# Five places for the short convolution of a hybrid decoder layer, and one sum taken from a transfer to VectorE

## The chip, the cores and the metric

The kernel runs on one core of a Trainium2 chip. The metric is the device time of one execution in microseconds (us), the median over several runs. Five engines work side by side: TensorE (PE in the profile, its weight loads PEld), VectorE (DVE), ScalarE (ACT), GpSimd (POOL) and SyncE (SP), which issues most transfers. Each engine works through its own instructions in the order in which the program wrote them; an instruction that waits holds up all that stands behind it on that engine.

## What is computed

One decoder layer over 256 positions of 2048 channels: a norm, a mixer, a second norm and a feed-forward part, with scales and shifts from a conditioning vector. The mixer's part that is changed here is the short gated convolution:

```python
proj = h @ w_in                      # cb, cc, cx, q, k, v, r, a_lr
y_conv = cb * causal_dwconv3(cc * cx, conv_w)
o = gla_chunked(q, k, v, log_a)      # gated linear attention
o = rmsnorm(o, gla_norm_w) * silu(r)
y = concat([y_conv, o]) @ w_out
```

`causal_dwconv3` adds, per channel, three taps: position t times w2, position t-1 times w1, position t-2 times w0.

## The kernel before

Matrix products are made in split precision: each fp32 weight tile `raw` that arrives is copied by ACT to a rounded tile `wh` (line 138), DVE subtracts to get the rest `wl` (line 143), and TensorE adds the products of the high and low parts. A *unit* is one weight tile with its products. `drive` walks through all units in one fixed order that is written out by hand. For unit i it issues: the steps hung on `early`; `prep` of unit i+2 (the transfer of its weights on SP, the `wh` copy on ACT); `low` of unit i+1 (the `wl` subtraction on DVE); the steps on `pre`; the products of unit i on TensorE (`mm`); the steps on `mid`; the sums of unit i-1's banks (`fin`, function `evac`); and the steps on `late`.

The products with `w_in` are made in four chunks of input channels. This case is about the last chunk and what follows, which the code calls `tail`: t0 to t17 are the units of the last `w_in` chunk, t18 to t25 and t26 to t33 those of `w_out`. Units t12, t13, t14 and t17 have two column tiles, the other `w_in` units here three. `wh` has 3 buffers, `wl` 3, `raw` 6: the `wh` copy for unit i+3 waits for the products of unit i.

In `tail` these steps share the engines:

- `evac` of the last chunk: a finished pair of column tiles is added to what the earlier chunks left in `proj`. Most pairs are added by DVE from the bank (line 443). Pairs of cc, cx and v go another way: ACT copies the bank to a tile `hf` (line 440) and POOL issues an adding transfer to `proj` (line 441). Pairs 9 and 10 (both of cx) are summed in t11. Pair 11 is summed in t14.
- The linear attention: one level of scores per unit; `outputs` on TensorE at the start of t15; `norms` at the end of t15, eight squares with sums on ACT (line 368, bank of 256 columns) and a square root (line 738) that needs a table load; `scaled` in the `pre` of t16, a reciprocal on DVE (line 743) and eight scaled copies on ACT (line 748).
- `conv_pair(i)`, i from 0 to 3, with u = 9, 12, 13, 15. At the end of unit u, `first`: cc times cx on DVE (line 551), then the two copies scaled by tap 2 on ACT (line 553). In the `pre` of u+1, `second`: four shifted multiply-adds on DVE (line 134, 128x255 and 128x254), the product with cb (line 560) and its rounded copy on ACT (line 562). At the end of u+1 (u+2 for i = 3), `third`: the low part on DVE (line 566).
- `mod_steps`: multiply-adds of conditioning weights on DVE (line 134 with `macc`, 128x2048), one in most units.
- From t17 on, `turn`, `gate` and `gate_low`, which bring the attention's output to the form that `w_out` needs.

In the `pre` of t16, `scaled` was hung before the convolution's step, and stands ahead of it. A convolution pair i is first used by unit t18+i.

Of the kernel before, what the change touches and what calls it, by code (L numbers as in the profile page):

```python
# [24 lines left out]
CHUNKS = (2, 4, 5, 5)  # L25
# [17 lines left out]
BY_DMA = ("cc", "cx", "v")  # L43
# [58 lines left out]
def layer_kernel(ctx: ExitStack, tc, x, c, w_mod, b_mod, mix_pre_w, mix_post_w, w_in, conv_w, gate_w2, gate_b,  # L102
                 gla_norm_w, w_out, ffn_pre_w, ffn_post_w, w_up, ffn_conv_w, w_down, ident_in, masks_in, out):
    nc = tc.nc
# [12 lines left out]
    def nm(s):  # L117
        uid[0] += 1
        return f"{s}_{uid[0]}"

    def slot(shape, dt=F32):
        return big.tile(shape, dt, tag="big", name=nm("big"))
# [10 lines left out]
    def stt(o, a, s, b, op0=ALU.mult, op1=ALU.add):  # L133
        nc.vector.scalar_tensor_tensor(o, a, s, b, op0=op0, op1=op1)  # L134
# [90 lines left out]
    def conv_c(k, o):  # L225
        return sv[:, 32 + k * 8 + o:33 + k * 8 + o]
# [175 lines left out]
    def hf_tile():  # L402
        return wts.tile([P, 2, T], F32, tag="hf", name=nm("hf"), bufs=NHF)
# [15 lines left out]
    proj = {}  # L419
# [7 lines left out]
    def evac(ci, pair, ps):  # L427

        name = names[pair // 2]
        if name not in proj:  # L430
            proj[name] = slot([P, 4, T])
        dst = proj[name][:, (pair % 2) * 2:(pair % 2) * 2 + 2, :]
        if pair not in written:
            written.add(pair)
            nc.scalar.activation(dst, ps, AF.Copy, scale=QS if name == "q" else 1.0)
        elif name == "q":
            stt(dst, ps, QS, dst)
        elif ci == len(CHUNKS) - 1 and name[:-1] in BY_DMA:
            away_sum = hf_tile()
            nc.scalar.copy(away_sum, ps)  # L440
            nc.gpsimd.dma_start(dst, away_sum, accum_op=ALU.add)
        else:
            nc.vector.tensor_add(dst, dst, ps)
# [33 lines left out]
    def in_units(ci):  # L477
# [16 lines left out]
        def unit(tiles, plain):  # L494
# [37 lines left out]
            def fin():  # L532
                for p in dict.fromkeys(nt // 2 for nt in tiles):
                    done[p] = done.get(p, 0) + sum(nt // 2 == p for nt in tiles)
                    if done[p] == 2 and p not in keep:
                        evac(ci, p, banks[p])
# [6 lines left out]
    mts = {}  # L543

    def conv_pair(i):

        s = slice((i % 2) * 2, (i % 2) * 2 + 2)

        def first():
            cb, cc, cx = (proj[n + str(i // 2)][:, s, :] for n in ("cb", "cc", "cx"))  # L550
            nc.vector.tensor_mul(cc, cc, cx)
            for j in range(2):
                nc.scalar.activation(cx[:, j, :], cc[:, j, :], AF.Copy, scale=conv_c(2, 2 * i + j))

        def second():
            cb, cc, cx = (proj[n + str(i // 2)][:, s, :] for n in ("cb", "cc", "cx"))
            for tap, d in ((1, 1), (0, 2)):
                for j in range(2):
                    stt(cx[:, j, d:], cc[:, j, :T - d], conv_c(tap, 2 * i + j), cx[:, j, d:])
            nc.vector.tensor_mul(cb, cb, cx)  # L560
            mts[i] = slot([P, 2, 2, T], F32R)
            nc.scalar.copy(mts[i][:, :, 0, :], cb)

        def third():
            cb = proj["cb" + str(i // 2)][:, s, :]
            nc.vector.tensor_sub(mts[i][:, :, 1, :], cb, mts[i][:, :, 0, :].bitcast(F32))

        return first, second, third


    flat = lambda a: a.rearrange("p h t -> p (h t)")
# [503 lines left out]
    for ci in range(1, len(CHUNKS)):  # L1075
        n, us = CHUNKS[ci], chunks[ci - 1]
# [20 lines left out]
    tail = chunks[-1] + owait  # L1097
# [48 lines left out]
    for e in range(4):  # L1146
        tail[GATE[e] - 1].late.append(lambda e=e: turn(e))
    for i, u in enumerate(CONV):
        c0, c1, c2 = conv_pair(i)
        tail[u].late.append(c0)  # L1150
        tail[u + 1].pre.append(c1)
        tail[u + (1 if i < 3 else 2)].late.append(c2)
    owait[8].late.append(warm_sqrt)
    for t in range(2):
        owait[XRE + t].late.append(lambda t=t: load_x(t))
# [212 lines left out]
def build(nc, tc_args=None, arrays=None):  # L1368
    import concourse.tile as _tile

    args = []
    for name, a in arrays.items():
        args.append(nc.dram_tensor(f"in_{name}_dram", a.shape, mybir.dt.from_np(a.dtype), kind="ExternalInput").ap())
    for i, (shape, dtype) in enumerate(_OUTS):
        args.append(nc.dram_tensor(f"out_{i}_dram", shape, getattr(mybir.dt, dtype), kind="ExternalOutput").ap())
    with _tile.TileContext(nc, **(tc_args or {})) as tc:
        with tc.manual_schedule():
            layer_kernel(tc, *args)
# [13 lines left out]
```

## Time and profile before

| | |
|---|---|
| time, median of 3 runs | 1212.24 us (1211.05 to 1212.39) |
| the profiled execution's own time | 1211.78 us |
| its span, first to last instruction | 1210.0 us |
| PE busy | 1173.6 us (97%) |
| DVE busy | 937.0 us (77%) |
| ACT busy | 579.2 us (48%) |
| POOL busy | 45.6 us (4%) |
| granted TensorE clock, mean | 0.999 |

A share of busy time says little here: the `tail` lies between some 241 and 448 us of the span, and what an edit there is worth shows only in the stretches of that part, in who waits for whom.

### The profile page before, as it was taken

The numbers are of one execution on the slowest core, as the hardware profiler recorded it, in microseconds if no ns is written. First come the engines' busy times: TensorE is split into PE (matmuls) and PEld (weight loads), VectorE is DVE, ScalarE is ACT, GpSimd is POOL, SyncE is SP. The second block draws the span as 40 slices with busy tenths as digits, with TensorE's granted clock in tenths as the row PEclk, the third lists the DMA queues.
The fourth block names the chain that finished last, engine by engine and source line by source line (L and its number), as shares of the span: only waits on it lengthen the run. The fifth ranks groups of instructions, "written<-read, shape, count | busy, mean of one in ns | idle before, by whom it ended". The sixth has DMA issues, their size and how long they took to land.

```text
span 1210.0 us, 17230 instructions
## 1 busy us (share of the span) xinstructions
PE 1173.6 (97%) x7038; PEld 1038.3 (86%) x7038; DVE 937.0 (77%) x946; ACT 579.2 (48%) x675; POOL 45.6 (4%) x64
## 2 busy tenths in 40 slices
PE   2999999999999999999999999999999999999997
PEld 1999999999987888888888888888888888888885
DVE  5989899999999778884598979797976664545463
ACT  5563423454573547344554544544544543443442
POOL 2000020001101001000000000000000000000000
PEclk9999999999999999999999999999999999999999
DMA  9999899998899877996566767768664675555522
GB/s 301 387 391 390 305 384 400 399 361 266 235 336 373 330 282 284 345 375 213 174 217 238 276 220 256 254 212 296 224 230 153 226 261 180 202 191 191 198 80 70
DMA packets 128463, 323.88 MB, mean 268 GB/s; under 512 B 8502, under 2 KB 34566, under 8 KB 118657
## 3 DMA queue, kind: packets, MB, share of 16 engines
q1 hardware_dynamic: 124048, 312.63, 72.2%
q0 software_dynamic: 4048, 10.08, 3.2%
q8 instruction: 55, 0.90, 0.3%
q14 instruction: 24, 0.19, 0.0%
q10 hardware_dynamic: 288, 0.07, 0.0%
HBM read 315.42 MB, written 4.19 MB: 264 GB/s over the span
## 4 chain that ended last, share of the span: by engine, by line
PE 87%; DVE 4%; DMA 4%; issue 3%; ACT 1%; POOL 0%; SPq 0%; DVEq 0%; ACTq 0%; POOLq 0%
PE ps L936 27%; PE ps L938 14%; PE ps L793 9%; PE ps L794 9%; PE ps L792 9%; PE ps L525 5%; PE ps L527 5%; PE ps L526 5%; DMA raw<-in_w_mod_dram 2%; DVE big L134 1%; DVE wl L143 1%; PE ps L296 1%; DMA big<-hf 1%; PE ps L463 1%; DVE macc L134 1%
## 5 line engine op out<-in xcount | busy, mean ns | idle before, releaser
L138 ACT CAST wh<-raw 128x2048 fp32r<-128x2048 f32 (+3 forms) x203 | 370.1, 1826 | 502.9 <-PE ps L936 187.3
L143 DVE TENSOR_TENSOR wl<-raw,wh 128x2048 fp32r<-128x2048 f32 (+3 forms) x203 | 443.3, 2186 | 147.7 <-ACT wh L138 147.6
L936 PE MATMUL ps<-big,wh 128*128 128x512 f32 x1400 | 494.9, 399 | 0.0
L938 PE MATMUL ps<-big,wl 128*128 128x256 f32 x1400 | 393.1, 281 | 0.0
L936 PEld LDWEIGHTS ps<-big,wh 128*128 128x128 f32 x1400 | 263.0, 188 | 64.7
L938 PEld LDWEIGHTS ps<-big,wl 128*128 128x128 f32 x1400 | 264.5, 189 | 0.0
L527 PE MATMUL ps<-big,wl 128*128 128x256 f32 x768 | 218.7, 285 | 3.0 <-DVE wl L143 2.9
L525 PE MATMUL ps<-big,wh 128*128 128x256 f32 x768 | 220.4, 287 | 0.2 <-ACT wh L138 0.2
L526 PE MATMUL ps<-big,wh 128*128 128x256 f32 x768 | 218.3, 284 | 0.0
L134 DVE SCALAR_TENSOR_TENSOR macc<-raw,c_act,macc 128x2048 f32<-128x2048 f32 (+1 forms) x96 | 199.9, 2083 | 2.8 <-DMA raw<-in_w_mod_dram 2.6
L792 PE MATMUL ps<-wh,big 128*128 128x512 f32 x456 | 178.4, 391 | 0.0
L793 PE MATMUL ps<-wl,big 128*128 128x512 f32 x456 | 177.7, 390 | 0.4 <-DVE wl L143 0.3
L794 PE MATMUL ps<-wh,big 128*128 128x512 f32 x456 | 177.5, 389 | 0.0
L527 PEld LDWEIGHTS ps<-big,wl 128*128 128x128 f32 x768 | 148.3, 193 | 3.9 <-DVE wl L143 3.9
L525 PEld LDWEIGHTS ps<-big,wh 128*128 128x128 f32 x768 | 148.4, 193 | 2.7 <-ACT wh L138 1.4
L526 PEld LDWEIGHTS ps<-big,wh 128*128 128x128 f32 x768 | 148.4, 193 | 0.0
L793 PEld LDWEIGHTS ps<-wl,big 128*128 128x128 f32 x456 | 85.6, 188 | 18.8 <-DVE wl L143 1.0
L794 PEld LDWEIGHTS ps<-wh,big 128*128 128x128 f32 x456 | 85.6, 188 | 17.9
L792 PEld LDWEIGHTS ps<-wh,big 128*128 128x128 f32 x456 | 85.6, 188 | 17.7 <-issue 0.2
L134 DVE SCALAR_TENSOR_TENSOR big<-big,fcw,big 128x254 f32<-128x254 f32 (+1 forms) x176 | 72.4, 489 | 0.0
L862 DVE TENSOR_TENSOR big<-big,ps 128x256 f32<-128x256 f32 x88 | 31.1, 417 | 48.0 <-ACT big L860 48.0
L882 ACT ACTIVATE big<-big,fcw 128x256 f32<-128x256 f32 x88 | 37.9, 516 | 16.2 <-DVE big L873 16.2
(199 smaller groups left out, 649.5 us busy)
## 6 DMA issues: line engine op xcount, KB each, us to landing
raw<-in_w_up_dram SPq DMA_DIRECT2D x88, 1024.0 KB, 5.6
raw<-in_w_mod_dram SPq DMA_DIRECT2D x64, 1024.0 KB, 7.4
raw<-in_w_down_dram SPq DMA_DIRECT2D x44, 1024.0 KB, 4.8
raw<-in_w_in_dram SPq DMA_DIRECT2D x28, 960.0 KB, 9.2
raw<-in_w_mod_dram SPq DMA_DIRECT2D x32, 640.0 KB, 7.8
raw<-in_w_out_dram SPq DMA_DIRECT2D x16, 1024.0 KB, 7.7
raw<-in_w_in_dram SPq DMA_DIRECT2D x12, 1024.0 KB, 8.7
raw<-in_w_mod_dram SPq DMA_DIRECT2D x22, 512.0 KB, 8.3
```

The source lines that it names most:

```text
L134: nc.vector.scalar_tensor_tensor(o, a, s, b, op0=op0, op1=op1)
L138: nc.scalar.copy(hi, raw)
L143: nc.vector.tensor_sub(lo, raw, hi.bitcast(F32))
L525: nc.tensor.matmul(ps, w[0][:, kk, cs], ht[:, k % 2, 0, :], start=st, stop=False)
L526: nc.tensor.matmul(ps, w[0][:, kk, cs], ht[:, k % 2, 1, :], start=False, stop=False)
L527: nc.tensor.matmul(ps, w[1][:, kk, cs], ht[:, k % 2, 0, :], start=False, stop=sp)
L792: nc.tensor.matmul(ps, a[:, i, 0, ts_], w[0][:, kk, ns], start=st, stop=False)
L793: nc.tensor.matmul(ps, a[:, i, 0, ts_], w[1][:, kk, ns], start=False, stop=False)
L794: nc.tensor.matmul(ps, a[:, i, 1, ts_], w[0][:, kk, ns], start=False, stop=sp)
L882: nc.scalar.activation(st["c"][:, o, :], st["u"][o], AF.Copy, scale=fcw[:, 2, ch + o:ch + o + 1])
L936: nc.tensor.matmul(pss[o], wh[:, kk, cs], h2[k // 2][:, k % 2, :, :], start=(first and kk == 0), stop=False)
L938: nc.tensor.matmul(pss[o][:, 1, :], wl[:, kk, cs], h2[k // 2][:, k % 2, 0, :], start=False, stop=(last and kk == 3))
```

## The change

The convolution's three steps become five. `first` keeps only the product of cc and cx. The two tap copies on ACT become `tap`, in the `pre` of u+1, ahead of `second`. The rounded copy on ACT becomes `high_part`, at the end of u+1. `third`, the low part, stands at the end of u+2 for all four pairs. And in the last chunk pair 10 is added by DVE from its bank, without the copy and the transfer.

```diff
-        elif ci == len(CHUNKS) - 1 and name[:-1] in BY_DMA:
+        elif ci == len(CHUNKS) - 1 and name[:-1] in BY_DMA and pair != 10:
...
             nc.vector.tensor_mul(cc, cc, cx)
+
+        def tap():
+            cc, cx = (proj[n + str(i // 2)][:, s, :] for n in ("cc", "cx"))
             for j in range(2):
                 nc.scalar.activation(cx[:, j, :], cc[:, j, :], AF.Copy, scale=conv_c(2, 2 * i + j))
...
             nc.vector.tensor_mul(cb, cb, cx)
+
+        def high_part():
             mts[i] = slot([P, 2, 2, T], F32R)
-            nc.scalar.copy(mts[i][:, :, 0, :], cb)
+            nc.scalar.copy(mts[i][:, :, 0, :], proj["cb" + str(i // 2)][:, s, :])
...
-        return first, second, third
+        return first, tap, second, high_part, third
...
-        c0, c1, c2 = conv_pair(i)
-        tail[u].late.append(c0)
-        tail[u + 1].pre.append(c1)
-        tail[u + (1 if i < 3 else 2)].late.append(c2)
+        first, tap, second, high_part, third = conv_pair(i)
+        tail[u].late.append(first)
+        tail[u + 1].pre += [tap, second]
+        tail[u + 1].late.append(high_part)
+        tail[u + 2].late.append(third)
```

## Rows read from the trace of the kernel before

**Rows 1.** The page's first part: busy time of each engine over the whole span, its share, and the number of instructions.

```profile
PE 1173.6 (97%) x7038; PEld 1038.3 (86%) x7038; DVE 937.0 (77%) x946; ACT 579.2 (48%) x675; POOL 45.6 (4%) x64
```

**Rows 2.** Busy time by stretch: the stretch and its length in us, then the busy time of each engine in it (with the count of instructions), the granted clock, the share of the transfer engines and GB/s.

```profile
337.00:349.00 12.00, 10.72 (x86) 10.41 (x85) 11.28 (x16) 9.97 (x25) 1.97 (x3) 1.00 0.92 306
349.00:362.00 13.00, 12.62 (x78) 10.83 (x77) 12.97 (x12) 10.16 (x15) 0.00 (x0) 1.00 1.01 396
362.00:385.00 23.00, 23.00 (x104) 18.59 (x103) 23.00 (x21) 11.51 (x10) 0.85 (x1) 1.00 0.99 362
```

**Rows 3.** TensorE in order of time, 343 to 362 us (start, duration, instruction, idle time before it and what ended it): the first two are the products that waited for the `wl` tiles of units t16 and t18; the third, from the chain of work that ended last, is the first of t19 that needs `wl`.

```profile
344.86 0.39 PE L527 MATMUL ps<-big,wl 128*128 128x256 f32 x1 [1.28 <-DVE wl L143]
...
354.90 0.50 PE L793 MATMUL ps<-wl,big 128*128 128x512 f32 x1 [0.34 <-DVE wl L143]
...
361.16 0.50 PE ps L793
```

**Rows 4.** VectorE in order of time, from 311 to 355 us, the instructions on which the sum rests. The three rows of line 143 are the `wl` tiles of t16, t17 and t18.

```profile
311.48 0.69 DVE L654 TENSOR_TENSOR big<-big 128x512 f32<-128x512 f32 x1
312.25 0.69 DVE L566 TENSOR_TENSOR big<-big,big 128x512 fp32r<-128x512 f32 x1
...
324.06 1.28 DVE L443 TENSOR_TENSOR big<-big,ps 128x512 f32<-128x512 f32 x2
326.85 0.69 DVE L551 TENSOR_TENSOR big<-big,big 128x512 f32<-128x512 f32 x1 [1.51 <-DMA big<-hf]
...
333.43 0.69 DVE L566 TENSOR_TENSOR big<-big,big 128x512 fp32r<-128x512 f32 x1
334.03 0.69 DVE L551 TENSOR_TENSOR big<-big,big 128x512 f32<-128x512 f32 x1
...
338.40 0.69 DVE L560 TENSOR_TENSOR big<-big,big 128x512 f32<-128x512 f32 x1
339.78 0.69 DVE L566 TENSOR_TENSOR big<-big,big 128x512 fp32r<-128x512 f32 x1 [0.69 <-ACT big L562]
...
342.66 2.15 DVE L143 TENSOR_TENSOR wl<-raw,wh 128x1920 fp32r<-128x1920 f32 x1
...
345.92 1.48 DVE L143 TENSOR_TENSOR wl<-raw,wh 128x1280 fp32r<-128x1280 f32 x1
347.32 0.20 DVE L743 RECIPROCAL grs<-grs 128x8 f32<-128x8 f32 x1
347.44 1.62 DVE L134 SCALAR_TENSOR_TENSOR big<-big,sv,big 128x255 f32<-128x255 f32 x4
352.56 2.29 DVE L143 TENSOR_TENSOR wl<-raw,wh 128x2048 fp32r<-128x2048 f32 x1
```

**Rows 5.** ScalarE in order of time, from 311 to 353 us. Line 138 is the `wh` copy: for t17 at 340.13, for t18 at 347.63.

```profile
311.60 0.62 ACT L562 CAST big<-big 128x512 fp32r<-128x512 f32 x1 [2.47 <-DVE big L560]
312.12 1.06 ACT L440 COPY hf<-ps 128x512 f32<-128x512 f32 x2
...
339.13 0.62 ACT L562 CAST big<-big 128x512 fp32r<-128x512 f32 x1 [1.78 <-DVE big L560]
339.66 0.58 ACT L440 COPY hf<-ps 128x512 f32<-128x512 f32 x1
340.13 1.27 ACT L138 CAST wh<-raw 128x1280 fp32r<-128x1280 f32 x1
341.30 0.38 ACT L368 ACTIVATE junk<-ps 128x256 bf16<-128x256 f32 x1
...
345.33 1.28 ACT L738 ACT_TABLE_LOAD   x1
346.63 0.30 ACT L738 ACTIVATE grs<-gss,eps_t 128x8 f32<-128x8 f32 x1
346.83 0.89 ACT L553 ACTIVATE big<-big,sv 128x256 f32<-128x256 f32 x2
347.63 1.90 ACT L138 CAST wh<-raw 128x2048 fp32r<-128x2048 f32 x1
349.43 3.01 ACT L748 ACTIVATE big<-ps,grs 128x256 f32<-128x256 f32 x8
352.29 0.66 ACT L562 CAST big<-big 128x512 fp32r<-128x512 f32 x1
```

**Rows 6.** The adding transfers: from the chain of work that ended last, the transfer of pair 9, from its issue to its landing; and from the view of line 441 between 270 and 360 us, the time from issue to landing over ten such transfers.

```profile
318.01 8.75 DMA big<-hf
...
DMA to landing us min/median/max: 3.3/6.0/10.6
```

**Rows 7.** Who waited for whom between 361 and 387 us (total us, times, longest): ScalarE's longest.

```profile
ACT big L763 <- DVE big L134: 7.8, 3, 3.5
```

**Rows 8.** The granted clock at both ends of the span: TensorE in order of time at 31 and 36 us, and busy time by stretch (columns as in Rows 2) at the end, where the three products of the first stretch are the last of the program.

```profile
31.33 0.58 PE L527 MATMUL ps<-big,wl 128*128 128x256 f32 x1 [0.74 <-DVE wl L143]
...
36.15 0.28 PE L525 MATMUL ps<-big,wh 128*128 128x256 f32 x1
...
1201.00:1206.80 5.80, 0.63 (x3) 0.19 (x1) 3.19 (x6) 1.70 (x4) 1.26 (x1) 1.00 0.35 116
1206.90:1210.00 3.10, 0.00 (x0) 0.00 (x0) 0.00 (x0) 0.00 (x0) 0.00 (x0) 0.50 0.33 111
```

## The prediction, made before the changed kernel was run

> **What bounds the kernel now.** The page comes first: PE is busy 97% of the span, DVE 77% [rows 1]. That is a mean; the change touches t9 to t17, so I next cut that part into stretches. From 337 to 349 us PE is idle for 1.28 us, from 349 to 362 for 0.38, and DVE has hardly a gap (11.28 of 12.00, 12.97 of 13.00), and none at all in the 23 us after that [rows 2]. PE in order of time names the idle: 1.28 us before a product of t16 and 0.34 before one of t18, both until DVE delivers `wl` [rows 3]. So here DVE's place in its own list sets the time, and what the change is worth is where DVE stands at the `wl` of t16 (342.66) and of t18 (352.56). All PE idle that such an edit could remove is 1.28 + 0.34, and some tenths at the neighbouring products. Then I read DVE's own order: before those two tiles it waits twice, 1.51 us at 326.85 for the adding transfer of pair 9, and 0.69 us at 339.78 for ACT's rounded copy [rows 4]. Last ACT's order: it stands 2.47 and 1.78 us at line 562 for DVE, with work behind that could run [rows 5].
>
> **The change part by part.** All times are the profiled execution's, clocked as in the rows; a step lasts from its start to the start of the next.
>
> *Pair 10 by DVE.* One more line 443, 0.60 us (start to start; the pair of them at 324.06 lasts 1.28 [rows 4]). It removes one `hf` copy on ACT (about 0.5 us, half of 1.06 [rows 5]) and one POOL issue; POOL is 4% busy [rows 1], so that is nothing. Without the wait DVE would have been at conv pair 1's product (line 551) at 326.85 - 1.51 = 325.34 [rows 4]. With the added sum it is 325.94. The low part of pair 0 (line 566) moves from t10 to t11, still ahead of this point, so its 0.6 us cancels; what goes is the 0.17 us that it stood at 312.25 (the instruction ahead started at 311.48 and takes 0.60 to the next). So 325.77.
>
> *Will pair 9 have landed?* Its ACT copy stood behind those of pairs 5 and 6, and these behind line 562, which waited 2.47 us for DVE [rows 5]. With line 562 moved behind them, pairs 5 and 6 leave some 3 us sooner. I put pair 9's issue near 315, not 318.01: its copy still waits for the rounded copy of pair 0, two decays and a `wh` copy. The old 8.75 us to landing gives 323.8, the worst of ten 10.6 gives 325.6 [rows 6]. I take it as landed: the 1.51 us go, 0.60 of it is filled by the added sum. If it isn't, DVE starts at 326.85 as before, 1.08 later than I count.
>
> *Low part a unit later.* DVE was at line 551 of pair 2 at 334.03, 7.18 us after that of pair 1; line 566 at 333.43 now stands after it, which saves 0.60 [rows 4]: 325.77 + 6.58 = 332.35. Line 560 of pair 2 came 4.37 us later (338.40), so 336.72. The wait of 0.69 us at line 566 is gone, since the low part that now stands there is pair 1's, whose copy is made a unit earlier. The `wl` of t16, at 342.66 before, then starts at 336.72 + 4.26 - 0.69 = 340.29, 2.4 us sooner, and PE's 1.28 us at t16 go [rows 3, 4]. That is the good half.
>
> *Taps behind the `wh` copy.* For pairs 0 to 2 the two tap copies now follow a `wh` copy. I cost that at nothing: between line 551 and the multiply-adds DVE has a `wl` subtraction of 1.4 to 2.1 us, and ACT starts its `wh` copy before line 551 is done, since it no longer stands there for it. Without that cover it would cost at most one `wh` copy, 1.9 us, each time, and nothing at the least [rows 5].
>
> *Taps of pair 3 behind the norm's scaled copies.* This is the term that decides. Pair 3 has u = 15, so its `tap` stands in the `pre` of t16, and there `scaled` was hung first. ACT before: square root 346.63, taps 346.83, `wh` of t18 at 347.63, eight scaled copies from 349.43 to 352.29 [rows 5]. ACT after: square root, `wh`, eight scaled copies, taps. DVE's multiply-adds, at 347.44 before [rows 4], must wait for the first tap. ACT's chain from line 560 of pair 2 runs, each step from [rows 5]: rounded copy at 336.72 + 0.73 = 337.45; the `hf` copy of pair 11 is already ahead of it, so `wh` of t17 at + 0.53 = 337.98; squares + 1.17 = 339.15; table load + 4.03 = 343.18; root + 1.30 = 344.48; `wh` of t18 + 0.20 = 344.68; scaled copies + 1.80 = 346.48; taps + 2.86 = 349.34; first tap done after half of its 0.89, and 0.05 to the release, some 349.85.
>
> DVE gets there sooner: from line 560 to the reciprocal were 8.92 us (338.40 to 347.32), less the 0.69 wait, plus one moved line 566 of 0.60 (pair 2's now stands in t15): 336.72 + 8.83 = 345.55. It then stands idle for 4.3 us, and starts the multiply-adds at 349.85, 2.4 us **later** than before. Queued behind them on DVE are line 560, a conditioning multiply-add, a bank sum and the `wl` of t18, without a gap in the old order (347.44 to 352.56). So that `wl` is done at 357.3, and PE's product of t18, at 354.90 before, starts there. Without the wait at t16 PE would be ready for it at 354.90 - 0.34 - 1.28 = 353.28, so PE stands for 4.0 us.
>
> *Is it won back?* No: from 349 to 385 DVE is full [rows 2], t19's first `wl` product already follows at once (361.16 [rows 3]), and in that part ACT's longest waits are for DVE [rows 7], no row naming a weight transfer. Weight transfers that SP issues when DVE frees a `raw` tile start 2.4 us later with it, and all their users too.
>
> **Sum.** + 2.4 us at t18, carried to the end: 1211.78 + 2.4 = 1214.2 for an execution like the profiled one, which was 0.46 us under the median. Against the median: 1214.7. Bounds of this case: 1.4 us if ACT's and DVE's chains run a microsecond tighter than their rows, 3.5 if pair 9 is late by its 1.08; so 1213.6 to 1215.8.
>
> **The clock.** At the end of the span the granted clock is 1.00 up to 1206.8 and 0.50 from 1206.9, with the last three products over soon after 1201 [rows 8]: standing idle, PE fell to its lower level (1.2 GHz) after some 5 us. No row shows what 4 us in mid-kernel do; the 1.28 us of [rows 3] left the clock at 1.00 [rows 2]. The Trainium skill (TensorE: Matmul & The Clock Gate, "Why this matters for your kernels") warns that idle gaps between bursts of products in mid-kernel can drop the clock to half. By that rule the change would cost more than DVE's delay. What that would be is rival A.
>
> **The rivals.**
> A. The clock falls in PE's 4 us of idle. At the start PE worked from 31.33 until its products got shorter at 36.15 [rows 8], 4.8 us at the lower level, which is 2.4 us of work lost. Then 1214.7 + 2.4 = 1217.1. For it: the end of the span. Against it: that idle was longer.
> B. Pair 9 lands late all the same (SP's weight transfers ride on the same transfer engines). Then all behind is 1.08 later, ACT's chain too: 1215.8. For it: the spread of 3.3 to 10.6 us [rows 6].
> C. The other side: ACT is through its chain before DVE needs the taps, and only the two removed waits count. It decides at 345.55: if the first tap is done by then, DVE is 1.89 us ahead of before, the `wl` of t18 is done at 352.96, PE takes it at 353.3 instead of 354.90, and the time is 1210.6. Against it: eight squares and eight scaled copies, 6.9 us, lie ahead of the taps and none can start before DVE's line 560. For it: ACT is under half busy [rows 1].
> D. Half-way: ACT's chain gains another 1 to 2 us (squares or copies closer together), gain and loss cancel, and the change moves the work but not the end: about 1212.9.
>
> **How the numbers follow.** Forecast 60%, A 15%, B 12%, C 7%, D 6%. This kernel's measurement tells 0.2%, 2.4 us, from nothing, so slower begins at 1214.66, right at the forecast: half of its 60, and all of A and B, give 57% slower; the rest of it, D and half of C (whose gain is under 2.4 by its sum) 39% the same, and half of C, 4%, faster. Range 1212.6 to 1217.6: it leaves out C and the upper part of A. The likeliest case's own range is the 1213.6 to 1215.8 above.
>
> **What would show it.** DVE's line 551 near 325.8 without a wait for a transfer; no PE wait at t16; on ACT line 553 right after the last line 748; on DVE a wait of about 4 us for line 553 ahead of the multiply-adds near 350; one PE wait of about 4 us for `wl` near 357; the clock in the stretch behind it. I am wrong if DVE shows no wait for line 553 in t16, or if PE's waits there and at t16 together come to less than 1.6 us.

## The result, and the profile after

The changed kernel takes 1216.05 us (median of 6 runs, 1214.88 to 1216.38) against 1211.41 us for the kernel before, measured again beside it (6 runs, 1210.67 to 1212.39). The ratio is 1.0036, 95% interval 1.0023 to 1.0049: it is slower by 4.4 us by this ratio, and by 4.6 us between the two medians. The profiled execution took 1216.0 us.

PE's waits in the whole span, of the kernel after (who waited for whom, total us, times, longest). The 12.2 and 10.4 us at the top are the start of the program, and were there before.

```profile
PE ps L381 <- DVE big L1057: 12.2, 2, 9.0
PE ps L220 <- DMA ident<-in_ident_dram: 10.4, 1, 10.4
PE ps L798 <- DVE wl L143: 4.0, 1, 4.0
```

There is one wait of 4.0 us that the kernel before didn't have. Line 798 is the `wl` product of `w_out` (793 before). Busy time by stretch, columns as in [rows 2], places it:

```profile
337.00:349.00 12.00, 12.00 (x98) 11.90 (x97) 8.45 (x9) 11.60 (x29) 1.10 (x2) 1.00 0.98 352
349.00:362.00 13.00, 8.97 (x46) 7.64 (x45) 12.36 (x13) 7.52 (x8) 0.00 (x0) 0.74 0.71 264
358.00:362.00 4.00, 4.00 (x11) 3.07 (x11) 4.00 (x4) 2.54 (x2) 0.00 (x0) 0.50 0.81 316
```

Read it against [rows 2]. From 337 to 349 PE has lost its idle time (12.00 of 12.00, 10.72 before), and it is DVE that now stands (8.45 busy, 11.28 before). From 349 to 362 PE is busy for 8.97 us instead of 12.62. And the seventh number, the granted clock, is 0.74 there, which was 1.00: in the third row, PE works without a gap, at 0.50. The share in the second row makes 0.26 x 13 / 0.5 = 6.8 us at the lower level.

DVE in order of time shows both halves of the change (line 563 is the old 560, 571 the old 566, 748 the old 743):

```profile
325.48 0.69 DVE L551 TENSOR_TENSOR big<-big,big 128x512 f32<-128x512 f32 x1
...
339.89 2.15 DVE L143 TENSOR_TENSOR wl<-raw,wh 128x1920 fp32r<-128x1920 f32 x1
...
343.73 0.69 DVE L551 TENSOR_TENSOR big<-big,big 128x512 f32<-128x512 f32 x1 [0.49 <-DMA big<-hf]
...
345.74 0.20 DVE L748 RECIPROCAL grs<-grs 128x8 f32<-128x8 f32 x1
349.61 1.67 DVE L134 SCALAR_TENSOR_TENSOR big<-big,sv,big 128x255 f32<-128x255 f32 x4 [3.67 <-ACT big L556]
...
354.78 2.28 DVE L143 TENSOR_TENSOR wl<-raw,wh 128x2048 fp32r<-128x2048 f32 x1
```

The wait for pair 9's transfer is gone (325.48, in [rows 4] 326.85 after 1.51 us). The `wl` of t16 starts at 339.89 instead of 342.66. Then the multiply-adds of pair 3 wait 3.67 us for line 556, the tap copies, and the `wl` of t18 starts at 354.78 instead of 352.56. ACT says why, first its order from the square root on, and then the chain of work that ended last, over the same time:

```profile
344.15 0.30 ACT L743 ACTIVATE grs<-gss,eps_t 128x8 f32<-128x8 f32 x1
344.36 1.90 ACT L138 CAST wh<-raw 128x2048 fp32r<-128x2048 f32 x1
346.16 3.02 ACT L753 ACTIVATE big<-ps,grs 128x256 f32<-128x256 f32 x8
349.02 0.95 ACT L556 ACTIVATE big<-big,sv 128x256 f32<-128x256 f32 x2
```

```profile
344.46 1.80 ACT wh L138
346.26 2.92 ACT big L753 x8
349.18 0.41 ACT big L556
...
349.61 1.68 DVE big L134 x4
...
354.78 2.29 DVE wl L143
...
357.12 0.80 PE ps L798
```

In [rows 5] the tap copies stood ahead of the `wh` copy and the eight scaled copies; here they stand behind both, and the chain that sets the end runs through all of it. On TensorE (products of 128x512 in t18) the lower clock is seen in the starts:

```profile
357.12 0.80 PE L798 MATMUL ps<-wl,big 128*128 128x512 f32 x1 [4.03 <-DVE wl L143]
...
358.56 0.63 PE L798 MATMUL ps<-wl,big 128*128 128x512 f32 x1
358.99 0.63 PE L799 MATMUL ps<-wh,big 128*128 128x512 f32 x1
...
361.97 0.41 PE L797 MATMUL ps<-wh,big 128*128 128x512 f32 x1
...
362.46 0.40 PE L799 MATMUL ps<-wh,big 128*128 128x512 f32 x1
362.70 0.39 PE L797 MATMUL ps<-wh,big 128*128 128x512 f32 x1
```

Two products are 0.43 us apart at 358.56, and 0.24 at 362.46.

### The profile page after: what moved, and what is told of

Read it like the earlier page. It is cut to its first block, busy times and chain, and to the rows that moved or that the text cites. A ratio compares the mean times of both kernels' runs of the same rounds, so it can differ in the third digit from the quotient of the medians.

```text
span 1214.2 us, 17225 instructions
## 1 busy us (share of the span) xinstructions
PE 1175.3 (97%) x7038; PEld 1039.3 (86%) x7038; DVE 937.5 (77%) x947; ACT 578.9 (48%) x674; POOL 44.7 (4%) x63
## 4 chain that ended last, share of the span: by engine, by line
PE 90%; DMA 4%; DVE 4%; ACT 1%; issue 1%; SPq 0%; DVEq 0%; ACTq 0%
PE ps L941 27%; PE ps L943 14%; PE ps L798 9%; PE ps L799 9%; PE ps L797 9%; PE ps L525 6%; PE ps L526 6%; PE ps L527 6%; DMA raw<-in_w_mod_dram 4%; DVE big L134 1%; PE ps L296 1%; PE ps L629 1%; DVE wl L143 1%; DVE macc L134 1%; PE ps L463 1%
```

## The experiments

Two theories. S: the loss is DVE's wait for pair 3's taps, which the change put behind the scaled copies, plus the clock that falls in PE's idle time. W: the spread itself costs, through one more sum on DVE and more waits. Each run was timed beside the kernel before, whose median in the three groups of runs was 1211.65 (first to fourth), 1211.67 (fifth to eighth) and 1211.63 us (the last two).

**1. The taps of pair 3 back at the end of t15.**

```diff
-        tail[u].late.append(first)
-        tail[u + 1].pre += [tap, second]
+        tail[u].late += [first, tap] if i == 3 else [first]
+        tail[u + 1].pre += [second] if i == 3 else [tap, second]
```

> The whole change, but pair 3's two tap copies stay at the end of t15, as before. Theory S (the loss is DVE's wait in t16 for tap copies that stand behind the scaled copies, and the clock that falls in PE's idle time after it): DVE's multiply-adds of pair 3 start near 346 instead of 349.6, PE waits under 1 us at t18, the clock stays at 1.00, and the gain of the other moves is kept: about 1209.8 us, 1.6 below before. Rival W (the spread itself costs: one more sum and more waits on DVE): most of the loss stays, 1214 us or more.

Measured: 1210.07 us, ratio 0.9986 (0.9977 to 0.9994). The whole loss is gone and the kernel is 1.6 us faster than before. DVE in order of time:

```profile
344.93 0.20 DVE L748 RECIPROCAL grs<-grs 128x8 f32<-128x8 f32 x1
345.05 1.62 DVE L134 SCALAR_TENSOR_TENSOR big<-big,sv,big 128x255 f32<-128x255 f32 x4
...
350.17 2.28 DVE L143 TENSOR_TENSOR wl<-raw,wh 128x2048 fp32r<-128x2048 f32 x1
```

The multiply-adds follow the reciprocal at once, and the `wl` of t18 is 2.4 us ahead of [rows 4]. All other edits are still in, so W falls.

**2. The taps in t16, but ahead of the scaled copies.**

```diff
-        tail[u + 1].pre += [tap, second]
+        if i == 3:
+            tail[u + 1].pre.insert(0, tap)
+            tail[u + 1].pre.append(second)
+        else:
+            tail[u + 1].pre += [tap, second]
```

> The whole change, but in the steps before the products of t16 pair 3's tap copies stand ahead of the eight scaled copies instead of behind them. Theory S: the taps still wait for the weight copy of t18 (1.8 us on ACT), so DVE's multiply-adds start near 346.7, 0.7 sooner than in the kernel before; PE waits some 1 us at t18, clock 1.00; about 1210.6 us. Rival W: 1214 us or more.

Measured: 1211.41 us, ratio 0.9997 (0.9989 to 1.0006), which can't be told from no change; I had expected 0.8 less. The mechanism is the expected one. DVE in order of time, and then PE's one wait at t18 in the view of waits:

```profile
346.62 1.67 DVE L134 SCALAR_TENSOR_TENSOR big<-big,sv,big 128x255 f32<-128x255 f32 x4 [1.30 <-ACT big L556]
```

```profile
PE ps L798 <- DVE wl L143: 1.1, 1, 1.1
```

Standing behind the `wh` copy alone costs 1.3 us of waiting on DVE, and that gives back most of what the other moves win.

**3. The kernel before, with that one move alone.**

```diff
             nc.vector.tensor_mul(cc, cc, cx)
+            if i < 3:
+                tap()
+
+        def tap():
+            cc, cx = (proj[n + str(i // 2)][:, s, :] for n in ("cc", "cx"))
             for j in range(2):
...
-        c0, c1, c2 = conv_pair(i)
+        c0, tap, c1, c2 = conv_pair(i)
         tail[u].late.append(c0)
+        if i == 3:
+            tail[u + 1].pre.append(tap)
```

> The kernel before with only pair 3's tap copies moved behind the scaled copies of t16. Theory S: without the gain of the other moves DVE's multiply-adds start near 352.0 instead of 347.4, 4.6 later, PE stands idle for some 4.9 us before t18 and the clock falls to 0.50 for some us: 1218 us; with the clock at 1.00 it would be 1216. Rival W: this one move is harmless, 1211 to 1212 us.

Measured: 1218.26 us, ratio 1.0054 (1.004 to 1.0067). DVE's multiply-adds in order of time, PE's wait at t18, and the stretch behind it (columns as in [rows 2]):

```profile
351.51 1.67 DVE L134 SCALAR_TENSOR_TENSOR big<-big,sv,big 128x255 f32<-128x255 f32 x4 [4.16 <-ACT big L558]
```

```profile
PE ps L798 <- DVE wl L143: 5.0, 1, 5.0
```

```profile
359.00:365.00 6.00, 5.97 (x14) 4.77 (x15) 6.00 (x5) 2.85 (x2) 0.00 (x0) 0.50 0.88 309
```

So this one move costs 6.6 us by itself. The rest of the change, taken together, wins back 1218.26 - 1216.05 = 2.2 of them.

**4. The idle time filled, so that the clock holds.** Added are 14 products whose sums are overwritten; nothing else changes.

```diff
                     pss.update({(t, n): bank([P, 512]) for t in range(2) for n in range(2)})
                 ws[k2] = cur["w"]
+                if nh == 0 and k2 == 0:
+                    for _ in range(14):
+                        nc.tensor.matmul(pss[0, 0], ones_r, cur["w"][0][:, 0, 0:512], start=True, stop=True)
```

> The whole change, with 14 products of 128x512 into a bank of t18, whose sums are overwritten, put between t17's and t18's products, so that PE has some 3 us of work in its 4 us of waiting. Theory S: DVE as in the changed kernel, the first wl product of t18 still near 357.1, but the clock stays at 1.00 and t18 runs at full pace: 1213.7 us, 2.3 below the changed kernel. Rival V (the clock's dip costs nothing here since DVE sets the pace behind it): 1216 us as without them.

Measured: 1214.02 us (1213.74 to 1214.61), ratio 1.002 (1.0011 to 1.0028). DVE still waits 4.0 us for the taps; PE is left with 0.8 us, and the clock in t18 is 1.00 (the waits from 300 to 400 us, then the stretch of t18):

```profile
DVE big L134 <- ACT big L556: 4.0, 1, 4.0
...
PE ps L798 <- DVE wl L143: 0.8, 1, 0.8
```

```profile
357.50:363.00 5.50, 5.50 (x25) 4.52 (x26) 5.50 (x5) 2.87 (x2) 0.00 (x0) 1.00 0.86 303
```

This splits the loss. Against the kernel before, DVE's lateness is 1214.02 - 1211.65 = 2.4 us; the clock is the other 1216.05 - 1214.02 = 2.0 us (2.3 if each time is first compared with the median of the kernel before beside it). The rival, that the dip costs nothing, falls.

**5. Useful work in the idle time.** In t18 and t19 the 16 products that need no `wl` come first, the 8 others last.

```diff
+                if nh == 0 and k2 < 2:
+                    for lo in (False, True):
+                        for k in (2 * k2, 2 * k2 + 1):
+                            a, w, i = mts[k2], cur["w"], k % 2
+                            for t in range(2):
+                                for n in range(2):
+                                    ts_, ns = slice(t * P, (t + 1) * P), slice(n * 512, (n + 1) * 512)
+                                    if lo:
+                                        nc.tensor.matmul(pss[t, n], a[:, i, 0, ts_], w[1][:, i, ns], start=False, stop=False)
+                                    else:
+                                        nc.tensor.matmul(pss[t, n], a[:, i, 0, ts_], w[0][:, i, ns], start=k == 0, stop=False)
+                                        nc.tensor.matmul(pss[t, n], a[:, i, 1, ts_], w[0][:, i, ns], start=False, stop=False)
+                    return
```

> The whole change, with the products of t18 and t19 in another order: first the 16 that don't need wl, then the 8 that do. Theory S: DVE unchanged, but PE has 3.7 us of work while it waits at t18, so the idle shrinks to under 1 us, the clock stays at 1.00, and what is left is DVE's own lateness, which shows at t20 (a wait of about 1 us): about 1211.3 us, as the kernel before. Rival L (DVE's 2.2 us of lateness stay in the end whatever PE does meanwhile): 1213.7 us, as with the filling products.

Measured: 1211.82 us, ratio 1.0002 (0.9993 to 1.0011). PE's waits from 345 to 400 us:

```profile
PE ps L798 <- DVE wl L143: 0.8, 1, 0.8
PE ps L840 <- DVE big L443: 0.7, 1, 0.7
```

The wait at t20 is there as expected, and one that I had not counted: the second row is a high product of t18 that waits for the DVE sum that frees its bank. The loss is gone although DVE is as late as in the changed kernel. Its `wl` of t18, in DVE's order of time, starts at 354.77, and at 354.78 there:

```profile
354.77 2.28 DVE L143 TENSOR_TENSOR wl<-raw,wh 128x2048 fp32r<-128x2048 f32 x1
```

So L falls: what costs time is PE's idle and the clock behind it, and DVE's lateness costs only as far as it makes PE stand. That the new order wins by itself, whatever DVE does, is the rival here; run 10 finds no such gain that its interval can tell.

**6. A shorter filling.** As the fourth, with 5 products instead of 14.

> The whole change, with 5 instead of 14 filling products, so that PE's wait at t18 is about 2.9 us. If idle time of that length leaves the clock at 1.00: 1214.0 us; if it still falls: 1216 us. Both theories leave it open; it bounds the idle time that costs the clock.

Measured: 1215.23 us (1214.02 to 1216.3), ratio 1.003 (1.0019 to 1.0041): neither of the two. The executions differ among themselves. Two of the seven have a granted clock of 0.999 over the whole run and took 1214.02 and 1214.43 us, within the times of run 4; the five others have 0.995 to 0.997 and took 1214.79 to 1216.3, more than any execution of run 4. The profiled one is the slowest of them, at 0.995: PE waited 3.0 us and the clock fell (the view of waits, then the stretch behind).

```profile
PE ps L798 <- DVE wl L143: 3.0, 1, 3.0
```

```profile
357.00:362.90 5.90, 5.90 (x14) 4.64 (x15) 5.90 (x5) 2.85 (x2) 0.00 (x0) 0.50 0.88 296
```

That the clock held in the two at 0.999 is inferred from their clock and time; the profile is of another execution.

**7. The change without the edit of pair 10**, and **8. that edit alone** on the kernel before.

```diff
-        elif ci == len(CHUNKS) - 1 and name[:-1] in BY_DMA:
+        elif ci == len(CHUNKS) - 1 and name[:-1] in BY_DMA and pair != 10:
```

> The whole change without its first edit: pair 10 goes by transfer again. Theory S: DVE saves the 0.60 us of the sum at t11, pair 9 still lands before DVE needs it since its copy is early, ACT's chain follows DVE, so the wait in t16 ends 0.6 us sooner: 1215.4 us. Rival P (pair 10's transfer was what made pair 9 late): DVE's wait for pair 9 near 326 is back, 1216 to 1217 us.

> The kernel before with only the edit of pair 10: summed by DVE. Theory S: pair 9's copy still stands behind ACT's wait at line 562, it lands near 326 to 327 as before, and the sum fills 0.6 of DVE's 1.51 us of waiting: no change, 1211.0 to 1211.7 us. Rival P (pair 10's transfer was what made pair 9 late): pair 9 lands 1 us or more sooner and PE's wait at t16 shrinks by it: 1210.5 us.

Measured: 1215.14 us without it (ratio 1.0029, 1.0018 to 1.0039), 1211.53 us with it alone (0.9999, 0.999 to 1.0008). The first row is DVE in order of time in the seventh run: no wait for a transfer, though pair 10's is back. The second is DVE in the eighth: the wait is there, 0.74 us of the 1.51, and the added sum fills most of the rest. The third and fourth are POOL's issue of pair 9's transfer, in the changed kernel and in the eighth run.

```profile
324.70 0.69 DVE L551 TENSOR_TENSOR big<-big,big 128x512 f32<-128x512 f32 x1
```

```profile
326.38 0.69 DVE L551 TENSOR_TENSOR big<-big,big 128x512 f32<-128x512 f32 x1 [0.74 <-DMA big<-hf]
```

```profile
315.21 0.85 POOL L441 DMA_DIRECT2D big<-hf  x1 [4.32 <-ACT hf L440]
```

```profile
317.73 0.86 POOL L441 DMA_DIRECT2D big<-hf  x1 [3.29 <-ACT hf L440]
```

Before, that issue was at 318.01 [rows 6], so the edit of pair 10 hardly moves it and the moves of the steps bring it 2.8 us forward. ACT's wait ahead of it for line 560, 2.47 us in [rows 5], is 0.46 us in the changed kernel. So pair 9's lateness came from ACT's order, not from pair 10, and P falls in both; no run moves the rounded copy without the taps. In the profile of the seventh run the clock's dip is only half as long as in the changed kernel:

```profile
356.10:359.40 3.30, 3.06 (x7) 2.48 (x8) 3.30 (x5) 2.48 (x2) 0.00 (x0) 0.50 0.96 367
359.50:365.00 5.50, 5.50 (x28) 4.53 (x27) 5.50 (x6) 2.02 (x4) 0.00 (x0) 1.00 0.85 299
```

This profile is of one of three executions at a granted clock of 0.997, which took 1214.47 to 1215.02 us; the four others, at 0.995, took 1215.14 to 1215.84. The 0.9 us between the seventh run and the changed kernel is therefore not all the 0.6 us of the sum; how much is the dip's length can't be told from these runs, and the intervals of the two ratios overlap.

**9. The first experiment without the edit of pair 10**, and **10. the first with the low products last**, as in the fifth.

> As the first experiment (the whole change, pair 3's tap copies at the end of t15), but pair 10 by transfer again: the moves of the steps alone. Theory S: DVE is 0.6 us further ahead, but there PE hardly waits for it any more (0.07 us at t19 in the first experiment), so nothing is won or lost: 1209.8 to 1210.2 us. Rival P (the gain of the first experiment is pair 10's): 1211 us or more.

> The first experiment with the wl products of t18 and t19 last. Theory S: DVE is no longer late there, so only some 0.3 us at t19 are left to win: 1209.7 to 1210.1 us. A rival to S would be a gain of over 1 us, which would say that DVE still holds up PE where the first experiment's profile shows no wait.

Measured: 1209.48 us (ratio 0.9982, 0.9973 to 0.9991) and 1209.65 us (0.9983, 0.9974 to 0.9992). They are 0.3 and 0.05 us under what I expected, which is less than these medians can tell; P falls. The ninth, in stretches:

```profile
337.00:349.00 12.00, 12.00 (x98) 11.87 (x98) 11.80 (x14) 11.75 (x30) 1.10 (x2) 1.00 0.99 360
349.00:362.00 13.00, 12.90 (x75) 11.08 (x74) 13.00 (x12) 9.60 (x11) 0.00 (x0) 1.00 0.98 375
```

PE has 0.10 us of idle left in the 25 us where it had 1.66 in [rows 2]. This version, the five places with pair 3's taps left in t15 and pair 10 left to the transfer, was the fastest measured, 2.1 us under the kernel before. It can't be told apart from the first and the tenth. In the traces the edit of pair 10 has a small price: every profile with it has, ahead of t16, a wait of PE for DVE that those without it don't have, as here in the first run (the waits from 240 to 400 us):

```profile
PE ps L629 <- DVE big L691: 0.2, 1, 0.2
```

## Why the prediction was right, point by point

The direction and the place were right, and the time lies in the range (1212.6 to 1217.6), which the forecast and rival A share. It is 1.35 us above the forecast of 1214.7, outside the likeliest case's own range (1213.6 to 1215.8), and 1.05 below rival A's 1217.1. What happened is the forecast's mechanism with rival A on top. The forecast looks nearer than it was, and that is luck: it stood on a median of 1212.24 us for the kernel before, and the six runs beside the changed kernel gave 1211.41. As a difference the forecast was 2.4 us and rival A 4.8; measured were 4.4 to 4.6.

- *What bounds the kernel* held: in runs 1 to 3, which move nothing but pair 3's taps (1 and 2 against the changed kernel, 3 against the kernel before), the time follows DVE's place at the `wl` of t18. Run 5 narrows it: that place costs time through PE's idle alone.
- *Pair 10 and pair 9's landing* held: DVE stood at line 551 at 325.48 without a wait (counted: 325.77). The reason given, the earlier copy, is shown by its issue at 315.21 (counted: near 315) and by runs 7 and 8; rival B is out.
- *Low part a unit later* held: the `wl` of t16 at 339.89 (counted: 340.29), and PE's wait there is gone.
- *Taps behind the `wh` copy*, put at nothing, held for pairs 0 to 2: from 300 to 400 us DVE waits for line 556 once only, in t16. Where the cover is missing, in run 2, the `wh` copy does cost a wait, of 1.3 us.
- *Taps of pair 3 behind the scaled copies* held: root 344.15 (344.48), multiply-adds 349.61 (349.85), and DVE stood 3.67 us where I counted 4.3. Part of the difference is a wait of 0.49 us for pair 11's transfer at 343.73, which I had not foreseen and which cost nothing, as DVE had to wait anyway. Rivals C and D are out with it.
- *Is it won back*: the answer, no, held, but the reason given was the wrong one. With the clock kept up, run 4 measured 2.4 us at the end, the sum's term. The prediction laid this to DVE, which is full from 349 to 385. In run 5 DVE is just as full and as late, and the loss is gone. What can't be won back is idle time of PE, which from 362 to 385 is as full as DVE (23.00 of 23.00 [rows 2]): in run 4 the 0.8 us that PE stands and the 3.35 us that the added products take, less the 1.28 + 0.34 before, make 2.5, nearly the 2.4 measured.
- *The clock* is the term that I mis-sized: in the sum it stood at nothing, in rival A at 2.4 us with a chance of 15%. It cost 2.0 us. In the profiled execution it fell; over the whole run the granted clock is 0.995 or 0.996 in four of the six, under all that the kernel before shows (0.997 to 0.999). The other two have 0.997, which run 8 also has in its profile without a dip in this part, so that number doesn't decide for them; both are slower than every execution of run 4. The argument against A, that the idle of 5 us at the end of the span was longer, was no argument: nothing in the rows said that 4 us are too short. A's price of 2.4 us came from the start of the program, where the profile's clock column reads 1.00; the lower level is inferred there from the products of 128x256, 0.21 us apart before 36.15 and 0.12 after. The rule cited from the Trainium skill (TensorE: Matmul & The Clock Gate, "Why this matters for your kernels"), that idle gaps in mid-kernel can drop the clock, is borne out here: 0.50 behind a gap of 4.03 us, 1.00 behind one of 0.8 in run 4. It deserved the larger chance.
- *The bound on the gain*, PE's 1.28 + 0.34 us of idle and some tenths, held as well: runs 1, 9 and 10 won 1.6 to 2.2. Of run 9's 2.15 us the idle time that is gone explains 1.56; the rest is less than its interval can tell.

## What to carry to other kernels

Before a step is moved on an engine, list what the new place has ahead of it in that engine's own order, not only what the step needs: here two copies, 0.9 us together, that DVE was about to need went behind 4.7 us of copies that were needed later. Where TensorE waits for several microseconds, price the lower clock behind the wait as well as the wait, and let products that need nothing late go first. When several small moves go together, run the one that the sum blames alone: here the rest of the change together was good, though one of its parts, the edit of pair 10, won nothing that a run could tell.

## What the runs showed of the hardware

An idle time of about 3 us before t18 cost the clock in some executions of one kernel and, by their clock and time, not in others (run 6, 0.995 to 0.997 in five and 0.999 in two); this was new to me. The time at the lower level differs between profiles as well: 6.8 us in the changed kernel, 3.3 in run 7, behind nearly the same idle time (4.0 and 3.9 us). And so does the moment at which the clock falls. The first row is from the changed kernel, where PE stood from 353.09, the second from run 3, where it stood from 353.99: in the stretch that begins some 3 us into the idle, the one has 0.50 and the other still 1.00.

```profile
356.00:357.00 1.00, 0.00 (x0) 0.00 (x0) 1.00 (x2) 0.00 (x0) 0.00 (x0) 0.50 0.96 324
```

```profile
357.00:358.00 1.00, 0.00 (x0) 0.00 (x0) 1.00 (x1) 0.66 (x1) 0.00 (x0) 1.00 0.83 139
```

What decides stays open. Also, a dip costs less than half its length, as part of it is idle. In the changed kernel 12 products lie between 357.12 and 361.97, 0.43 us apart for the most part; at the 0.24 seen afterwards they would take 2.9 us instead of 4.85, an estimate of 2.0 us lost, the same that run 4 measured.
